# A trunk layer's first projections on one core: the first adaLN columns computed by TensorE, six places for w_ada, smaller first blocks, and ScalarE copies out of PSUM

## The chip, the cores and the metric

The kernel runs on one core of one Trainium2 chip. Its time is the device time of one execution in microseconds (us); the figure given is the median of three. Engines are named as in the profile: PE is TensorE's matmul, PEld its weight load, DVE is VectorE, ACT ScalarE, POOL GpSimd and SP SyncE, which here issues the loads.

## The reference, cut to what matters

The layer takes x (512 rows of 2048) and one conditioning vector c of 2048. Scale and shift columns come from c, and everything starts from them:

```python
cond = silu(c)
mod = cond @ w_ada + b_ada                  # 6 vectors of 2048
sh1, sc1, g1, sh2, sc2, g2 = split(mod, 6)
u = x * (1 + sc1) + sh1
proj = u @ w_in                             # 2048 -> 6168 columns: GLA and mLSTM
...                                         # the two head groups, w_out, LayerNorm, MLP, LayerNorm
```

Both head groups, the output projection and the MLP follow; the change doesn't touch them.

## The kernel before, in words

All matrices are f32. To keep precision, an operand is split into a high part (rounded to the reduced f32 format, tile names ending in h) and a low part (the remainder, ending in l), and a product is three matmuls: high by high, low by high, high by low.

The first stage computes five groups of 512 output columns (gla q, gla k, two halves of gla v, mLSTM q; numbered g = 0 to 4) while the adaLN columns are still being made. The contraction over 2048 is cut into 16 steps k of 128, and these into blocks, `KBLOCKS = (1, 2, 3, 4, 4, 2)`. The fifth group takes part in the first `XBLOCKS = 3` blocks (k = 0 to 5) only. For each block the kernel needs sc1 and sh1 for the block's k, so it works as follows, in the order in which it is written:

- `ada_start` loads the block's columns of x into one of the y tiles, and rows of the transposed w_ada: for each k and each of sc1 and sh1 two tiles of 128x1024. These go through `ring_b`, a ring of `RING = 4` places, three loads ahead. `ada_sum` (line 162) multiplies such a tile by silu(c), which `csb` holds in all 128 partitions, and sums along the row, on VectorE. `mod_cols` (lines 168 and 169) adds halves and bias for the whole block.
- `x_T` transposes x on TensorE; `u_tile` makes u^T on ScalarE (uf, line 341; its high part uh, line 125) and its low part ul on VectorE (line 126).
- `start_unit` loads a unit of w_in (two k of one group, 128x2x512; one k where a block is odd) into one of three places, has ScalarE cast it (line 138) and GpSimd make the low part (line 139): the split. The raw place is free when the split is done.
- TensorE multiplies a unit into four PSUM banks of the group; six banks rotate. After a block's last unit of a group, `start_evac` empties the banks. For the first block it copies to SBUF (ScalarE, for g = 3 VectorE, line 652); for later blocks VectorE adds the bank to what is in SBUF (line 654), 20 adds of 128x512 in a block of five groups, 16 in one of four.

In this stage ScalarE, VectorE and SP keep the order in which the code is written; TensorE and GpSimd get theirs from a scheduler when the program is built. The steps of the next block's `ada_start` are spread over the units of the block that runs, and the code ahead of the last unit finishes them, so that every u tile of a block waits for the sums of all of its k.

Loads of the gate columns and their split stand at the blocks that `GBLOCK` names, and are at k = 3 and k = 6 before and after the change within one block. Behind this stage come the other projections (`group`), with the GLA work between.

Of the kernel before, what the change touches and what calls it, by code (L numbers as in the profile page):

```python
# [33 lines left out]
KBLOCKS = (1, 2, 3, 4, 4, 2)  # L34
XBLOCKS = 3
KX = sum(KBLOCKS[:XBLOCKS])
GBLOCK = 2
# [21 lines left out]
def trunk_layer_kernel(  # L59
    ctx: ExitStack, tc: tile.TileContext,  # L60
    x, c, w_ada, b_ada, w_in, w_alpha, b_alpha, gla_g, conv_w, conv_b,
# [283 lines left out]
    def ada_start(k0, nk):  # L345
        xb = y[1 + len(xbn) % 3].rearrange("p (t c) -> p t c", c=CB)
        nc.sync.dma_start(xb[:, :, :nk * P], xr[:, :, k0 * P:(k0 + nk) * P])
        xbn.append(k0)
        xbs.update((k0 + i, (xb, i)) for i in range(nk))
        todo = [(v, k, h) for k in range(k0, k0 + nk) for v in (SC1, SH1) for h in range(2)]  # L350
        raws = [ada_load(*u) for u in todo[:RING - 1]]
        yield
        for i, u in enumerate(todo):
            ada_sum(raws.pop(0), *u)
            if i + RING - 1 < len(todo):
                raws.append(ada_load(*todo[i + RING - 1]))
            yield
        mod_cols(slice(SH1, SC1 + 1), k0, nk)
# [281 lines left out]

    def start_evac(i, g, j, bank):
# [1008 lines left out]
```

## Time and profile before

| what | us |
| --- | --- |
| median of three executions (2177.06 to 2185.43) | 2181.04 |
| the profiled execution | 2177.7 |
| its span, first to last instruction | 2176.0 |
| TensorE busy in it | 2116.9 |
| VectorE busy | 1753.3 |
| ScalarE busy | 949.7 |
| GpSimd busy | 164.7 |

The profile shows one execution. An engine's busy time is an average over stages with different limits: what a change in one stage can be worth is to be looked for in the idle time of TensorE in that stage. The granted clock of TensorE is given as a share of its full speed.

### The profile page before, as it was taken

The page shows a single profiled execution, that of the slowest core. Times are in us where ns is not written, and L with a number is a line of the kernel's source. Part 1 is how long each engine was busy: PE and PEld are TensorE (multiplying, and loading weights), DVE is VectorE, ACT ScalarE, POOL GpSimd, SP SyncE. Part 2 cuts the span into 40 slices and gives each one's busy share as a digit, 9 for nine tenths or more (in the row PEclk, how much of TensorE's full clock was granted, in tenths as well). Part 3 has the DMA queues.
Part 4 walks back from the last instruction along what each step waited for, and adds up shares of the span by engine and source line. Part 5 has one row for each costly group of instructions (what it writes and reads, how often), then busy time and mean ns, then how long its engine had stood idle before and what let it go on. Part 6 is the DMA issues. An engine that isn't in the chain of part 4 may idle for free.

```text
span 2176.0 us, 34974 instructions
## 1 busy us (share of the span) xinstructions
PE 2116.9 (97%) x13873; PEld 1929.2 (89%) x13873; DVE 1753.3 (81%) x2802; ACT 949.7 (44%) x1343; POOL 164.7 (8%) x151
## 2 busy tenths in 40 slices
PE   6989999999999999999999999999999999999997
PEld 4767788888887878999999999998999999998885
DVE  7986777677776878988788788789898988885888
ACT  4222644243332136454444454455555555554223
POOL 3334100000000000000000000000001001011002
PEclk9999999999999999999999999999999999999999
DMA  8885444666668857444444444355556766779852
GB/s 311 274 279 185 126 138 149 224 227 218 216 233 301 284 198 233 136 138 143 127 131 133 125 137 135 117 161 180 198 168 169 197 165 172 193 185 270 284 189 82
DMA packets 187087, 409.79 MB, mean 188 GB/s; under 512 B 17440, under 2 KB 19708, under 8 KB 186924
## 3 DMA queue, kind: packets, MB, share of 16 engines
q1 hardware_dynamic: 180588, 387.38, 54.6%
q0 software_dynamic: 6336, 20.19, 5.3%
q8 instruction: 108, 1.77, 0.3%
q14 instruction: 55, 0.45, 0.1%
HBM read 354.74 MB, written 52.71 MB: 187 GB/s over the span
## 4 chain that ended last, share of the span: by engine, by line
PE 74%; DVE 13%; DMA 8%; ACT 2%; issue 2%; POOL 0%; SPq 0%; ACTq 0%; DVEq 0%; POOLq 0%
PE fp L1362 8%; PE fp L1361 8%; PE fp L1363 8%; PE gp L1434 7%; PE gp L1435 7%; PE gp L1436 7%; DVE wr L162 3%; DMA wr<-in_w_ada_dram 3%; DMA f<-in_w_ff_dram 2%; PE wo_0b L228 1%; PE wo_0b L230 1%; PE wo_0b L229 1%; DMA q<-sums 1%; PE mv0b L228 1%; PE gr0b L228 1%
## 5 line engine op out<-in xcount | busy, mean ns | idle before, releaser
L162 DVE SCALAR_TENSOR_TENSOR wr<-wr,csb 128x1024 f32<-128x1024 f32 x192 | 255.5, 1352 | 25.8 <-DMA wr<-in_w_ada_dram 25.6
L1164 DVE TENSOR_TENSOR z<-f 128x512 f32<-128x512 f32 x208 | 142.4, 685 | 0.2 <-DMA f<-in_w_ff_dram 0.2
L1460 POOL DMA_DIRECT2D sums<-z x33 | 28.5, 867 | 1110.3 <-DVE f_10lo L1198 802.2
L1166 DVE TENSOR_TENSOR z<-f,z 128x256 f32<-128x256 f32 x208 | 88.4, 425 | 7.2
L1167 DVE TENSOR_TENSOR z<-f,z 128x256 f32<-128x256 f32 x208 | 88.4, 425 | 7.2
L1387 ACT ACTIVATE z<-z 128x1024 f32<-128x1024 f32 x28 | 28.1, 1052 | 58.1 <-DVE z L1382 58.1
L1457 ACT COPY z<-gp 128x512 f32<-128x512 f32 x90 | 45.5, 603 | 5.8 <-DMA sums<-z 4.8
L1194 ACT CAST f_6hi<-z 128x1024 fp32r<-128x1024 f32 x18 | 18.9, 1052 | 39.3 <-DVE z L1167 39.3
L1198 DVE TENSOR_TENSOR f_0lo<-z,f_0hi 128x1024 fp32r<-128x1024 f32 x17 | 20.8, 1226 | 18.5 <-ACT f_0hi L1194 18.5
L1194 ACT CAST f_4hi<-z 128x1024 fp32r<-128x1024 f32 x18 | 19.1, 1059 | 33.8 <-DVE z L1167 33.8
L1194 ACT CAST f_0hi<-z 128x1024 fp32r<-128x1024 f32 x17 | 17.8, 1050 | 33.3 <-PE fp L1362 24.5
L654 DVE TENSOR_TENSOR gqk<-gqk,st 128x512 f32<-128x512 f32 x40 | 25.3, 680 | 7.5 <-PE st L223 7.4
L1198 DVE TENSOR_TENSOR f_1lo<-z,f_1hi 128x1024 fp32r<-128x1024 f32 x14 | 17.2, 1226 | 17.6 <-ACT f_1hi L1194 17.6
L654 DVE TENSOR_TENSOR gv<-gv,st 128x512 f32<-128x512 f32 x40 | 25.2, 679 | 6.3 <-PE st L230 6.3
L832 ACT ACTIVATE y<-mo,dd 128x256 f32<-128x256 f32 x16 | 7.6, 475 | 51.9 <-DVE dd L825 51.9
L1391 ACT ACTIVATE z<-z 128x1024 f32<-128x1024 f32 x28 | 28.0, 1049 | 0.0
L1194 ACT CAST f_5hi<-z 128x1024 fp32r<-128x1024 f32 x14 | 14.7, 1051 | 30.4 <-DVE z L1167 30.4
L1194 ACT CAST f_1hi<-z 128x1024 fp32r<-128x1024 f32 x14 | 14.7, 1049 | 29.7 <-PE fp L1362 24.5
L1194 ACT CAST f_7hi<-z 128x1024 fp32r<-128x1024 f32 x14 | 14.7, 1050 | 28.8 <-PE fp L1362 24.4
L1198 DVE TENSOR_TENSOR f_6lo<-z,f_6hi 128x1024 fp32r<-128x1024 f32 x18 | 22.1, 1226 | 5.8 <-ACT f_6hi L1194 5.8
L1198 DVE TENSOR_TENSOR f_2lo<-z,f_2hi 128x1024 fp32r<-128x1024 f32 x18 | 22.1, 1225 | 5.8 <-ACT f_2hi L1194 5.8
L126 DVE TENSOR_TENSOR ul<-uf,uh 128x512 fp32r<-128x512 f32 x16 | 11.9, 752 | 18.2 <-ACT uh L125 18.2
(1914 smaller groups left out, 9015.6 us busy)
## 6 DMA issues: line engine op xcount, KB each, us to landing
f<-in_w_ff_dram SPq DMA_DIRECT2D x232, 512.0 KB, 3.8
wr<-in_w_ada_dram SPq DMA_DIRECT2D x192, 512.0 KB, 4.8
sums<-z POOLq DMA_DIRECT2D x33, 512.0 KB, 9.3
hd<-z SPq DMA_DIRECT2D x32, 512.0 KB, 4.0
z<-hd SPq DMA_DIRECT2D x28, 512.0 KB, 4.8
q<-sums SPq DMA_DIRECT2D x28, 256.0 KB, 5.9
sums<-z SPq DMA_DIRECT2D x12, 512.0 KB, 4.6
z<-in_x_dram SPq DMA_DIRECT2D x4, 1024.0 KB, 5.1
```

The costliest lines, as they stand in the source:

```text
L162: V.scalar_tensor_tensor(raw, raw, 1.0, csb[:, h * DH:(h + 1) * DH], ALU.mult, ALU.mult, accum_out=msum[:, h, v * KT + k:v * KT + k + 1])
L1164: V.tensor_tensor(halves(f[:, :S]), halves(raw[:, HB:3 * HB]), b12.unsqueeze(1).to_broadcast([P, 2, HB]), ALU.add)
L1166: V.tensor_tensor(t2, b22, n1, ALU.add)
L1167: V.tensor_tensor(t4, b21, t2, ALU.add)
L1194: A.copy(th, f)
L1198: V.tensor_tensor(tl, f, th, ALU.subtract)
L1361: T.matmul(o, lhsT=wh[:, sl], rhs=q[:, 0], start=i == 0 and j == 0, stop=False)
L1362: T.matmul(o, lhsT=wh[:, sl], rhs=q[:, 1], start=False, stop=False)
L1363: T.matmul(o, lhsT=wl[:, sl], rhs=q[:, 0], start=False, stop=i == KP - 1 and j == 1)
L1434: T.matmul(o, lhsT=qh[:, sl], rhs=wh, start=first and j == 0, stop=False)
L1435: T.matmul(o, lhsT=qh[:, sl], rhs=wl, start=False, stop=False)
L1436: T.matmul(o, lhsT=ql[:, sl], rhs=wh, start=False, stop=last and j == 1)
```

## The change

Five things change, all in the first stage.

1. The columns for k = 0 come from TensorE. The host passes `w_first`, the 2x128 columns of w_ada (not transposed) that give sh1 and sc1 for k = 0. c is loaded as 16 rows of 128, transposed, and passed through silu to `cs`; `ada_first` then does 2 x 16 plain f32 matmuls with one moving column each, and one VectorE add of the bias. `csb` is loaded later, behind the first two weight units, by `load_c`.
2. w_ada tiles have six places instead of four: `ring_s` adds two halves of the tile y[3], and five loads run ahead instead of three. x then uses two of the y tiles instead of three.
3. `KBLOCKS` becomes (1, 1, 2, 2, 4, 4, 2) with `XBLOCKS = 4`: k = 0 to 5 are four blocks instead of three, and five groups with 20 adds are emptied once more.
4. In all blocks but the first and the last, and for all groups but the block's last, ScalarE copies a bank into an SBUF tile (se, from the ring of `TB = 6` places that uf uses too), and VectorE adds that tile later (`start_adds`, line 677), ahead of the next unit's matmuls in the order of the code. 72 such copies are made.
5. `GBLOCK` becomes 3, which keeps the gate loads near the same k.

```diff
-KBLOCKS = (1, 2, 3, 4, 4, 2)
-XBLOCKS = 3
+KBLOCKS = (1, 1, 2, 2, 4, 4, 2)
+XBLOCKS = 4
...
-GBLOCK = 2
+GBLOCK = 3
...
+    rows_c = const.tile([KT, P], F32, name="rows_c")
+    nc.sync.dma_start(rows_c, c.rearrange("o (j p) -> (o j) p", p=P))
+    ctp = aux_bank("ctp")
+    T.transpose(ctp[:, :KT], rows_c, ident[:KT, :KT])
+    cs = const.tile([P, KT], F32, name="cs")
+    A.activation(cs, ctp[:, :KT], AF.Silu)
     csb = side.tile([P, D], F32, name="csb")
     DH = D // 2
-    for h in range(2):
-        nc.sync.dma_start(csb[:, h * DH:(h + 1) * DH],
-                          c[0:1, h * DH:(h + 1) * DH].broadcast_to([P, DH]))
-        A.activation(csb[:, h * DH:(h + 1) * DH], csb[:, h * DH:(h + 1) * DH], AF.Silu)
+
+    def load_c():
+        for h in range(2):
+            sl = slice(h * DH, (h + 1) * DH)
+            nc.sync.dma_start(csb[:, sl], c[0:1, sl].broadcast_to([P, DH]))
+            A.activation(csb[:, sl], csb[:, sl], AF.Silu)
...
-    def ada_load(v, k, h):
-        raw, r0 = ring_b(f"wr{v}_{k}_{h}"), (v * KT + k) * P
+    def ada_load(v, k, h, raw=None):
+        raw, r0 = raw or ring_b(f"wr{v}_{k}_{h}"), (v * KT + k) * P
...
-    def ada_start(k0, nk):
-        xb = y[1 + len(xbn) % 3].rearrange("p (t c) -> p t c", c=CB)
+    def x_load(k0, nk):
+        xb = y[1 + len(xbn) % 2].rearrange("p (t c) -> p t c", c=CB)
...
+    def ada_first():
+        tp, raws = aux_bank("mp"), []
+        for r in range(4):
+            raw = ring_b(f"wf{r}").rearrange("p (t c) -> p t c", c=2 * P)
+            nc.sync.dma_start(raw, w_first[r * CB:(r + 1) * CB].rearrange("(t p) c -> p t c", p=P))
+            raws.append(raw)
+        for v in range(2):
+            for k in range(KT):
+                T.matmul(tp[:, v:v + 1], lhsT=raws[k // 4][:, k % 4, v * P:(v + 1) * P],
+                         rhs=cs[:, k:k + 1], start=k == 0, stop=k == KT - 1)
+        V.tensor_tensor(mod[:, 0:2 * KT:KT], tp[:, :2], cA[:, 0:2 * KT:KT], ALU.add)
...
+    def ring_s():
+        ringn.append(len(ringn) % 6)
+        i = ringn[-1]
+        return y[3][:, (i - 4) * DH:(i - 3) * DH] if i > 3 else None
+
+    def ada_start(k0, nk):
+        x_load(k0, nk)
         todo = [(v, k, h) for k in range(k0, k0 + nk) for v in (SC1, SH1) for h in range(2)]
-        raws = [ada_load(*u) for u in todo[:RING - 1]]
+        raws = [ada_load(*u, ring_s()) for u in todo[:5]]
         yield
         for i, u in enumerate(todo):
             ada_sum(raws.pop(0), *u)
-            if i + RING - 1 < len(todo):
-                raws.append(ada_load(*todo[i + RING - 1]))
+            if i + 5 < len(todo):
+                raws.append(ada_load(*todo[i + 5], ring_s()))
             yield
...
+    adds = []
+
+    def start_adds():
+        while adds:
+            o, tmp = adds.pop(0)
+            V.tensor_tensor(o, o, tmp, ALU.add)
+
...
         if i == 0:
             (V.tensor_copy if g == 3 else A.copy)(o, src)
+        elif g == groups(i) - 1 or i == len(blocks) - 1:
+            V.tensor_tensor(o, o, src, ALU.add)
         else:
-            V.tensor_tensor(o, o, src, ALU.add)
+
+            tmp = tt2k(f"se{i}_{g}_{j}")
+            if 2 <= g < 4:
+                tmp = heads(tmp)
+            A.copy(tmp, src)
+            adds.append((o, tmp))
...
-    gen = ada_start(*blocks[0])
-    next(gen)
+    x_load(*blocks[0])
     tps = [x_T(k, mm_bank) for k in range(KBLOCKS[0])]
-    for _ in gen:
-        pass
+    ada_first()
     start_unit(0)
     start_unit(1)
+    load_c()
     for k, tp in enumerate(tps):
         u_tile(k, tp)
...
         for _ in range(share):
             next(gen, None)
+        start_adds()
```

Three places in the order of instructions. The first is ScalarE at the very start, up to the high part of the first u; cs is the small silu, csb the silu over all partitions, sw_0 the first weight units. Before:

```order
L98 ACT_TABLE_LOAD
L98 ACTIVATE csb<-csb 128x1024 x2
L138 CAST sw_0h<-sw_0r 128x512 x2
L341 ACTIVATE uf_170<-up_145,mod 128x512
L125 CAST uh_172<-uf_170 128x512
```

Now:

```order
L97 ACT_TABLE_LOAD
L97 ACTIVATE cs<-ctp 128x16
L145 CAST sw_0h<-sw_0r 128x512 x2
L105 ACTIVATE csb<-csb 128x1024 x2
L348 ACTIVATE uf_204<-up_141,mod 128x512
L132 CAST uh_206<-uf_204 128x512
```

The two passes over csb moved from the front to behind the first two weight casts, and still stand ahead of uf.

The second is VectorE where mod for k = 6 to 9 is made, at the end of the block with k = 5; gv is the running sum of the value projection, ul the low parts for k = 6 to 9. Before:

```order
L162 SCALAR_TENSOR_TENSOR wr_9_1_845,msum<-wr_9_1_845,csb 128x1024
L168 TENSOR_TENSOR mod<-msum 128x2x4
L169 TENSOR_TENSOR mod<-mod,cA_c 128x2x4
L126 TENSOR_TENSOR ul_944<-uf_941,uh_943 128x512
L126 TENSOR_TENSOR ul_955<-uf_952,uh_954 128x512
```

Now:

```order
L175 TENSOR_TENSOR mod<-msum 128x2x4
L176 TENSOR_TENSOR mod<-mod,cA_c 128x2x4
L677 TENSOR_TENSOR gv_104<-gv_104,se_2_0_1019 128x2x256
L677 TENSOR_TENSOR gv_105<-gv_105,se_2_1_1021 128x2x256
L677 TENSOR_TENSOR gv_106<-gv_106,se_2_2_1023 128x2x256
L677 TENSOR_TENSOR gv_107<-gv_107,se_2_3_1025 128x2x256
L677 TENSOR_TENSOR gv_104<-gv_104,se_3_0_1069 128x2x256
L677 TENSOR_TENSOR gv_105<-gv_105,se_3_1_1071 128x2x256
L677 TENSOR_TENSOR gv_106<-gv_106,se_3_2_1073 128x2x256
L677 TENSOR_TENSOR gv_107<-gv_107,se_3_3_1075 128x2x256
L133 TENSOR_TENSOR ul_1089<-uf_1086,uh_1088 128x512
```

The adds of groups 2 and 3 now stand between mod and the first ul; before, those groups were added ahead of mod.

The third is ScalarE inside a block (before the one with k = 3 to 5, now the one with k = 2 and 3); sw_2, sw_3, sw_4 and sw_5 are weight units, se the new SBUF tiles. Before:

```order
L125 CAST uh_583<-uf_581 128x512
L138 CAST sw_5h<-sw_5r 128x512
L138 CAST sw_3h<-sw_3r 128x1024
L138 CAST sw_5h<-sw_5r 128x512
L138 CAST sw_3h<-sw_3r 128x1024
```

Now:

```order
L145 CAST sw_2h<-sw_2r 128x1024
L698 COPY se_1_0_681<-st_1_0_653 128x512
L698 COPY se_1_1_683<-st_1_1_654 128x512
L698 COPY se_1_2_685<-st_1_2_655 128x512
L698 COPY se_1_3_687<-st_1_3_656 128x512
L145 CAST sw_2h<-sw_2r 128x1024
L698 COPY se_2_0_730<-st_2_0_702 128x512
```

Between two casts of weight units there are now four copies out of PSUM. Behind the first stage the instructions of each engine stand in the order in which they stood.

## Rows read from the trace of the kernel before

**Rows 1.** The page's head, and the busy time of each engine.

```profile
span 2176.0 us, 34974 instructions
PE 2116.9 (97%) x13873; PEld 1929.2 (89%) x13873; DVE 1753.3 (81%) x2802; ACT 949.7 (44%) x1343; POOL 164.7 (8%) x151
```

**Rows 2.** Busy us by stretch: PE, PEld, DVE, ACT, POOL; then PEclk, DMA share, GB/s.

```profile
0.00:18.23 18.23, 1.51 (x5) 0.90 (x5) 7.56 (x14) 6.08 (x8) 4.68 (x20) 1.00 0.92 332
...
18.23:124.06 105.83, 93.81 (x396) 73.94 (x397) 93.61 (x126) 34.76 (x52) 41.40 (x19) 0.97 0.84 285
124.06:179.80 55.74, 52.03 (x230) 39.26 (x229) 46.89 (x65) 17.33 (x23) 24.24 (x10) 1.00 0.78 270
...
179.80:227.00 47.20, 47.20 (x214) 38.19 (x213) 25.29 (x34) 12.51 (x15) 20.36 (x9) 1.00 0.38 122
```

**Rows 3.** Timeline up to the first projection: start, duration, instruction, idle before.

```profile
6.65 1.06 ACT L98 ACTIVATE csb<-csb 128x1024 f32<-128x1024 f32 x1 [0.74 <-DMA csb<-in_c_dram]
...
13.45 1.29 ACT L138 CAST sw_0h<-sw_0r 128x512 fp32r<-128x512 f32 x2 [5.74 <-DMA sw_0r<-in_w_in_dram]
...
16.75 0.78 ACT L341 ACTIVATE uf<-up,mod 128x512 f32<-128x512 f32 x1 [2.01 <-DVE mod L169]
...
18.23 0.80 PE L221 MATMUL st<-uh,sw_0h 128*128 128x512 f32 x1 [9.45 <-ACT uh L125]
```

**Rows 4.** Weight loads of transposes (ns min/median/max), and one plain f32 matmul's pair.

```profile
L335 PEld LDWEIGHTS up<-ident,y x20: 139/141/230, 7.7 to 46.4; 128*128 128x128 f32 x20
...
267.67 0.33 PE L577 MATMUL gs<-y,k 128*64 128x64 f32 x2
```

**Rows 5.** VectorE from 40.9 to 120 us: busy, mean ns, idle before.

```profile
L162 DVE SCALAR_TENSOR_TENSOR wr<-wr,csb 128x1024 f32<-128x1024 f32 x28 | 47.2, 1721 | 5.8 <-DMA wr<-in_w_ada_dram 5.8
L654 DVE TENSOR_TENSOR gv<-gv,st 128x512 f32<-128x512 f32 x16 | 9.9, 677 | 0.0
L654 DVE TENSOR_TENSOR gqk<-gqk,st 128x512 f32<-128x512 f32 x16 | 9.9, 675 | 0.0
L168 DVE TENSOR_TENSOR mod<-msum 128x6 f32<-128x6 f32 (+1 forms) x2 | 4.4, 2214 | 0.1
L654 DVE TENSOR_TENSOR y<-y,st 128x512 f32<-128x512 f32 x4 | 2.5, 681 | 0.0
...
L126 DVE TENSOR_TENSOR ul<-uf,uh 128x512 fp32r<-128x512 f32 x3 | 2.0, 688 | 0.6 <-ACT uh L125 0.6
```

**Rows 6.** Lines 654 and 162: ns min/median/max, first and last start.

```profile
L654 DVE TENSOR_TENSOR gqk<-gqk,st x40: 674/679/689, 46.5 to 241.8; 128x512 f32<-128x512 f32 x40
...
L162 DVE SCALAR_TENSOR_TENSOR wr<-wr,csb x28: 1211/1214/3409, 40.9 to 116.2; 128x1024 f32<-128x1024 f32 x28
```

**Rows 7.** Timeline of VectorE at single places.

```profile
40.91 1.22 DVE L162 SCALAR_TENSOR_TENSOR wr<-wr,csb 128x1024 f32<-128x1024 f32 x1 [2.50 <-DMA wr<-in_w_ada_dram]
...
46.55 2.47 DVE L654 TENSOR_TENSOR gqk<-gqk,st 128x512 f32<-128x512 f32 x4
48.94 1.21 DVE L162 SCALAR_TENSOR_TENSOR wr<-wr,csb 128x1024 f32<-128x1024 f32 x1
50.08 1.21 DVE L162 SCALAR_TENSOR_TENSOR wr<-wr,csb 128x1024 f32<-128x1024 f32 x1
...
121.44 0.69 DVE L126 TENSOR_TENSOR ul<-uf,uh 128x512 fp32r<-128x512 f32 x1 [1.55 <-ACT uh L125]
...
164.32 0.17 DVE L169 TENSOR_TENSOR mod<-mod,cA_c 128x8 f32<-128x8 f32 x1
```

**Rows 8.** SP's timeline between the first and the second wave of w_ada loads.

```profile
25.50 8.12 SPq L130 DMA_DIRECT2D sw_1r<-in_w_in_dram  x3
```

**Rows 9.** Timeline of TensorE: after a wait, and at k = 6.

```profile
56.40 0.80 PE L228 MATMUL st<-sw_1h,uh 128*128 128x512 f32 x1 [3.37 <-DVE gqk L654]
...
59.55 0.46 PE L229 MATMUL st<-sw_1l,uh 128*128 128x512 f32 x1
...
124.06 0.40 PE L221 MATMUL st<-uh,sw_6h 128*128 128x512 f32 x1
```

More of the change, by code (lines that the diff above doesn't have):

```diff
@@ L60, in trunk_layer_kernel @@
     ctx: ExitStack, tc: tile.TileContext,
-    x, c, w_ada, b_ada, w_in, w_alpha, b_alpha, gla_g, conv_w, conv_b,
+    x, c, w_ada, w_first, b_ada, w_in, w_alpha, b_alpha, gla_g, conv_w, conv_b,
     b_i, b_f, ml_g, w_out, ln1_g, ln1_b, w_ff1, w_ff2, ln2_g, ln2_b, out,
@@ L349, in ada_start @@
         xbs.update((k0 + i, (xb, i)) for i in range(nk))
+    def ada_first():
[9 more added lines that the diff above has]
+        V.tensor_tensor(mod[:, 0:2 * KT:KT], tp[:, :2], cA[:, 0:2 * KT:KT], ALU.add)
+    ringn = []
+    def ring_s():
[4 more added lines that the diff above has]
+        x_load(k0, nk)
         todo = [(v, k, h) for k in range(k0, k0 + nk) for v in (SC1, SH1) for h in range(2)]
-        raws = [ada_load(*u) for u in todo[:RING - 1]]
+        raws = [ada_load(*u, ring_s()) for u in todo[:5]]
         yield
@@ L1619, in trunk_layer_kernel @@
     f1p.release()
-_INS = ["x", "c", "w_ada", "b_ada", "w_in", "gla_w_alpha_up", "gla_b_alpha", "gla_norm_g",
+_INS = ["x", "c", "w_ada", "w_first", "b_ada", "w_in", "gla_w_alpha_up", "gla_b_alpha", "gla_norm_g",
         "mlstm_conv_w", "mlstm_conv_b", "mlstm_b_i", "mlstm_b_f", "mlstm_norm_g", "w_out",
         "ln1_g", "ln1_b", "w_ff1", "w_ff2", "ln2_g", "ln2_b"]
-_DROP = ("x", "w_ada", "w_in", "gla_w_alpha_up", "mlstm_conv_w", "w_out", "w_ff1", "w_ff2")
+_DROP = ("x", "w_ada", "w_first", "w_in", "gla_w_alpha_up", "mlstm_conv_w", "w_out", "w_ff1", "w_ff2")
 def kernel(**inputs):
@@ L1635 @@
     for name in _INS:
-        a = np.asarray(inputs[name])
+        a = np.asarray(inputs["w_ada" if name == "w_first" else name])
         if name in _DROP:
@@ L1640 @@
             a = a.T
+        if name == "w_first":
+            a = np.concatenate([a[:, :P], a[:, SC1 * D:SC1 * D + P]], 1)
         a = np.ascontiguousarray(a)
```

## The prediction, made before the changed kernel was timed

> **What bounds the kernel now.** I read the page's head first, then busy time by stretch, then the timelines of the stretches in which TensorE is not full. The profiled execution took 2177.7 us, its span is 2176.0 us, and TensorE is busy for 97% of it [rows 1]. No change can give more than the stretch that it touches loses, so the stretches come next [rows 2]. I cut them where TensorE takes up a new block of the contraction: 18.23 (k = 0), 124.06 (k = 6, the first matmul with tile sw_6h [rows 9]) and 179.80 (k = 10). Up to 18.23 TensorE has 1.5 us of work. From 18.23 to 124.06 it has 93.81 us of work in 105.83, from 124.06 to 179.80 52.03 in 55.74, and from 179.80 to 227 it is full: a loss of 16.7, 12.0, 3.7 and 0 us. The change rewrites only these stretches; the instructions behind them stand in the same order on every engine.
>
> The middle loss belongs to VectorE. It is busy 93.61 of the 105.83 us [rows 2]. There TensorE waits because VectorE, which works strictly in order, has not yet multiplied out the adaLN columns of the next block (the sums, line 162) or has not yet emptied a PSUM bank (the adds, line 654). What counts is when VectorE finishes mod for k = 6 to 9: in the kernel before 119.89, which is the start of ul at 121.44 less its wait of 1.55 [rows 7].
>
> **The start.** In the kernel before, the loads land in the order of their issue: both halves of csb (1.05 MB) by 6.65, the first weight tile by 13.45 when 3.67 MB have landed [rows 3], so 2.62 MB in 6.8 us, 0.385 MB a microsecond. In the changed kernel the four w_first tiles end at 2.41 MB: 6.65 + 1.36/0.385 = 10.2. Two chains then lead to the first projection.
> - *The columns.* The matmuls of ada_first run through all k for the first column, then again for the second. When the last tile lands, 4 + 16 matmuls are left. A matmul of plain f32 is two passes (a pair of records for one of line 577), and with one moving column a pass is little more than its load of 128 weight columns, of which the first transposes show 0.139 to 0.230 us [rows 4]. Forty passes are 5.6 to 9.2 us, so the sums are ready at 15.8 to 19.4. With 0.25 us for the add and 1.48 us from uf to the first matmul (16.75 to 18.23 [rows 3]) TensorE starts at 17.5 to 21.1.
> - *ScalarE's order.* The two passes over csb now stand ahead of uf, and csb lands behind 3.98 MB: 13.45 + 0.31/0.385 = 14.3. With 1.06 us for its last pass and 1.48 as above, 16.8.
>
> The first chain ends last. I take 18.5, nearer to its low end since 24 passes run ahead of those forty and may have brought the engine to its fast clock: no gain against 18.23. The Trainium skill (TensorE: Matmul & The Clock Gate, section LDWEIGHTS) has the load of 128 weight columns at 0.107 us whatever streams through them. By that the forty passes take 4.3 us, an estimate from that page, and the start would be 16.8, set by csb; the trace's weight loads here are 139 to 230 ns.
>
> **VectorE's ledger up to mod for k = 6 to 9.** In both kernels VectorE's steady work begins with the sums of the second load wave. Before, that is 40.91, after a wait of 2.50 [rows 7]: SP stood at three weight tiles for 8.12 us, until 33.62, and issued those w_ada loads behind them [rows 8], so they landed 7.3 us after it came free. What SP stands for is the GpSimd split of block 0's fifth unit. Afterwards that unit's load no longer queues behind busy w_ada buffers, and the split ends once TensorE is through two groups and ScalarE has copied and cast: 8 to 10 us after TensorE's start, 26.5 to 28.5, and with 7.3 33.8 to 35.8: **34.5** (31 to 36). Prices: a sum 1.14 us from start to start (48.94 to 50.08), four adds 2.39 (46.55 to 48.94), 0.60 each [rows 7].
> - *Before*, 40.91 to 119.89, 79.0 us [rows 5]: 28 sums, 32; 36 adds (16 + 16 + 4), 21.6; 3 ul, 2.0; 2 mod pairs, 0.7; waits 5.8 + 0.6. What is left, 17 us, is stall: the 28 sums took 47.2 us where 28 of 1.21 are 34.0, and the two mod adds 4.4 where undisturbed ones take 0.2 each. A stalled sum lasts up to 3.41 us [rows 6], 2.1 more than a free one, once for almost each of GpSimd's splits of 128x1024 that runs beside it.
> - *After*, the same point: 32 sums (blocks k = 2, 3; 4, 5; 6 to 9), 36.6; **48 adds** (20 + 20 + 8: the finer blocks empty the banks one round more often), 28.8; 4 ul, 2.6; 3 mod pairs, 1.0. That is 69.0 against 56.3.
> - *Stalls after*: 10 splits of 128x1024 (those of blocks k = 2, 3 and 4, 5) fall in this time, at 2.05 us 20.5; four of 128x512 are left out (up to 1 us each). The row for line 654 tells what is new here: an add with one operand in PSUM was never stalled (674 to 689 ns in 40 [rows 6]), and SBUF-only operations were. The change makes 40 of the 48 adds SBUF-only. If they stay free as before, stalls fall only on the sums, 36.6/(36.6 + 28.8) of 20.5: 11. I take 20.5, since a two-SBUF operand is what sums and adds then share. The Trainium skill (GPSIMD Engine Reference, section 1) says the same: GpSimd's SBUF interfaces are shared with VectorE and contend with instructions that read two SBUF inputs. By that rule the sum stands at 20.5; without it, it would be 11, and this rule speaks against the fourth part of the change.
> - *Waits after*: six places instead of four let SP run ahead, but the first wave is paced by landings: 3 (0 to 8).
>
> 34.5 + 69.0 + 20.5 + 3 = **127.0** for mod, against 119.9. From mod to the first ul VectorE then has eight adds first (two groups are pending, as the order rows show): 4.8 + 0.7, so TensorE starts k = 6 in earnest at 132.5. Before it started at 124.06, without a wait. That is **+8.4**.
>
> **After k = 6.** TensorE lost 3.7 us here. The adds for groups 0 to 2 no longer hold a bank: 12 copies of 0.6 us go to ScalarE, which is busy 17.33 of 55.74 [rows 2], and the six SBUF places behind the six banks cover the eight or nine sums in front of an add. **-3.7.** For k = 10 the lateness goes no further: before, its mod was there at 164.49 [rows 7], 15 us ahead of TensorE at 179.80. A gap of some us ahead of k = 6 also lowers TensorE's clock: after the wait that ended at 56.40 seven matmuls took 3.15 us to start where 1.6 is usual [rows 9], **+1.5**. ScalarE's 72 new copies (0.6 us each, 43 us up to k = 14) cost nothing: it works 52 of the 161 us up to 179.80; without that cover they would cost those 43. The loads of x into two buffers instead of three, the c rows and the late csb load cost nothing, being behind or ahead of loads that VectorE reaches later.
>
> **Sum**: 8.4 - 3.7 + 1.5 = +6.2 on the profiled execution's 2177.7, 2184. The median shown, 2181.0, is 3.3 above it, and the prediction is for a median: **2187 us**. A difference below 0.5% (10.9 us) is about what a measurement of this kernel can't tell from no change.
>
> **Rivals.**
> 1. *The ledger holds* (0.58): +6, 2187; its own range 2178 to 2196.
> 2. *The adds don't meet the splits* (0.20). Stalls 11, waits 0, start 33: mod at 113, TensorE at k = 6 at 118.5, that is -5.6; with -3.7, 2172. For it: the adds come in fours just after ScalarE's copies, and the split for the next group starts at about the same time and is soon over. Against it: SBUF-only ul and gw rows are stalled now. TensorE's own work forbids more than 18.5 + 93.8 = 112.3, -11.8 - 3.7, 2165.
> 3. *A loop closes, and it is slower* (0.22). ScalarE's copy waits for one of six SBUF places, so for VectorE's add; the cast of the next weight tile stands behind the copy, GpSimd's split behind the cast, SP's next weight load behind the split, and the next block's w_ada loads behind that. Before, no cast stood behind an add of VectorE on ScalarE's queue. It decides once VectorE runs so late that those loads land after it wants them; I put the slack at 4 us at k = 4 to 9. Price of one turn: the SP stand of 8.12 us [rows 8]. Mod at 135, TensorE at k = 6 at 140.5: +16.4 - 3.7 + 1.5 = +14, 2195. For it, VectorE is late by 7 already; against it, six places hold a group and a half.
>
> **The numbers.** The likeliest case gives 2187. The lower bounds together (31 + 69 + 11 + 0) and the upper ones (36 + 69 + 25 + 8 = 138, +17 in all) are unlikely to meet. The range that leaves out 2 in 10 is 2172 to 2200. Faster by over 0.5% needs 2170, the outer half of rival 2: 0.08. Slower by over 0.5% needs 2192: most of rival 3 and the upper tail of the ledger, 0.26. Within: 0.66.
>
> **What would show it.** Right: the first projection near 18.5; 108 adds in all on VectorE, and long ones (over 1 us) among those that read se tiles; mod for k = 6 to 9 near 127; TensorE idle ahead of k = 2, 4 and 6 with VectorE's ul as the one that ends it; no PSUM waits from there to k = 10. Wrong: adds on se tiles all near 680 ns (rival 2); ScalarE's copies waiting for adds, then SP for GpSimd's splits, then VectorE for w_ada (rival 3); a first projection after 21, with one-column passes above 0.23 us, which would move everything behind it; or TensorE waiting for ScalarE's casts between groups, which I have not priced.

## The result, and the profile after

The changed kernel took 2195.99 us (median; 2194.66 to 2197.50) against 2181.04 before: the ratio is 1.0075, 95% interval 1.0062 to 1.0087, so 16.4 us slower (13.5 to 19.0), clear of the 0.5% bound. The two medians as they stand differ by 15.0, which lies inside that interval. The prediction was 2187 in 2172 to 2200: the range holds it, the sign is right, and the time is 9 us above it. Its profiled execution has a span of 2195.2, 19.2 above that of before; that of before was 3.3 us under its median and this one 1.0 above, so the difference of these two executions overstates the change by about 4 us. The first fence is the page's head and the busy time by engine, the second the same view as [rows 2], cut where TensorE takes up k = 0, 6, 10 and 14.

```profile
span 2195.2 us, 35231 instructions
...
PE 2133.6 (97%) x13938; PEld 1946.2 (89%) x13938; DVE 1769.9 (81%) x2815; ACT 988.5 (45%) x1416; POOL 167.4 (8%) x151
```

```profile
0.00:22.68 22.68, 16.32 (x73) 15.23 (x73) 0.69 (x5) 6.26 (x9) 4.71 (x20) 1.00 0.81 268
22.68:140.08 117.40, 96.81 (x393) 76.68 (x394) 108.71 (x149) 59.67 (x100) 41.58 (x19) 0.94 0.79 277
140.08:197.04 56.96, 51.18 (x230) 39.59 (x228) 54.16 (x65) 22.86 (x34) 27.70 (x10) 1.00 0.71 249
197.04:244.26 47.22, 47.22 (x214) 38.22 (x212) 26.57 (x34) 19.25 (x27) 19.27 (x8) 1.00 0.30 91
```

Against [rows 2] the first projection is 4.45 us later (22.68 for 18.23), k = 6 is 16.0 later (140.08 for 124.06), k = 10 17.2 (197.04 for 179.80); the next stretch is as long as before. The loss lies ahead of k = 6, where VectorE is busy 108.71 of 117.40 us. The last 2 us of the 19.2 lie behind k = 14, in work that the change doesn't touch: 1950.9 us here, 1949.0 before, and 1945.5 (a_coarse) to 1952.5 (a_nofirst) in kernels below that have the same code there. So 2 us lie within what single executions show, and I don't explain them.

The start: TensorE's and its weight loads' timeline from 7 us on, then the instructions up to the first projection.

```profile
7.15 13.73 PEld L367 LDWEIGHTS mp<-cs,wf 128*128 128x128 f32 x64 [1.85 <-issue]
7.18 13.78 PE L367 MATMUL mp<-cs,wf 128*128 128x1 f32 x64 [1.48 <-DMA wf<-in_w_first_dram]
...
15.88 5.45 SPq L165 DMA_DIRECT2D wr<-in_w_ada_dram  x4
...
21.01 0.16 DVE L369 TENSOR_TENSOR mod<-mp,cA_c 128x2 f32<-128x2 f32 x1 [16.87 <-PE mp L367]
21.20 0.78 ACT L348 ACTIVATE uf<-up,mod 128x512 f32<-128x512 f32 x1 [4.50 <-DVE mod L369]
...
22.68 0.80 PE L228 MATMUL st<-uh,sw_0h 128*128 128x512 f32 x1 [0.97 <-ACT uh L132]
...
24.53 8.81 SPq L137 DMA_DIRECT2D sw_1r<-in_w_in_dram  x3
```

The 64 one-column passes run back to back from 7.15 to 20.9, 13.73/64 = 0.215 us each. No load paces them once the first tile is there. SP meanwhile stands 5.45 us, until 21.33, because these tiles hold four of the w_ada places, and the next weight loads go out behind that. It stands again until 33.34 for the split of a weight tile, ahead of the second wave's loads.

VectorE's timeline at the places of [rows 7]: the first sum of the second wave, and mod for k = 6 to 9 and k = 10 to 13.

```profile
41.16 1.77 DVE L169 SCALAR_TENSOR_TENSOR y<-y,csb 128x1024 f32<-128x1024 f32 x1 [2.94 <-DMA y<-in_w_ada_dram]
...
133.64 0.17 DVE L176 TENSOR_TENSOR mod<-mod,cA_c 128x8 f32<-128x8 f32 x1
...
184.02 0.17 DVE L176 TENSOR_TENSOR mod<-mod,cA_c 128x8 f32<-128x8 f32 x1
```

VectorE by line, from its first sum of the second wave to mod for k = 6 to 9 (the view of [rows 5]):

```profile
L169 DVE SCALAR_TENSOR_TENSOR wr<-wr,csb 128x1024 f32<-128x1024 f32 x20 | 34.3, 1759 | 0.0
L169 DVE SCALAR_TENSOR_TENSOR y<-y,csb 128x1024 f32<-128x1024 f32 x12 | 19.2, 1622 | 4.1 <-DMA y<-in_w_ada_dram 4.1
L677 DVE TENSOR_TENSOR gqk<-gqk,se 128x512 f32<-128x512 f32 x24 | 17.1, 771 | 0.0
L677 DVE TENSOR_TENSOR gv<-gv,se 128x512 f32<-128x512 f32 x16 | 14.2, 956 | 0.0
L692 DVE TENSOR_TENSOR y<-y,st 128x512 f32<-128x512 f32 x8 | 4.9, 670 | 0.0
```

And the lengths of the adds of line 677 in all (ns, minimum, median, maximum, as in [rows 6]), with who waited for them:

```profile
L677 DVE TENSOR_TENSOR gqk<-gqk,se x40: 676/679/2864, 47.4 to 219.6; 128x512 f32<-128x512 f32 x40
L677 DVE TENSOR_TENSOR gv<-gv,se x32: 677/682/2896, 58.1 to 230.5; 128x512 f32<-128x512 f32 x32
...
who waited for it (us, times):
  ACT se L698: 18.6, 6
```

The forecast's ledger can be read off: 32 sums and 24 + 16 + 8 = 48 adds, as counted. Nine sums lasted 1.77 to 3.42 us, 15.8 more than nine of 1.21; three of the 40 adds on se tiles 2.86 to 2.90, 6.6 more in all: stalls of 22 us. The adds on se tiles do meet the splits; the eight that read PSUM (line 692) show no stall.

What TensorE waited for, up to 320 us (total, times, longest):

```profile
PE st L235 <- ACT se L698: 8.6, 2, 4.4
PE up L342 <- ACT uf L348: 6.9, 3, 4.0
PE st L228 <- ACT uh L132: 5.2, 3, 3.2
...
PE st L236 <- POOL sw_6l L146: 2.0, 1, 2.0
PE st L228 <- ACT se L698: 1.9, 3, 1.4
PE st L229 <- DVE ul L133: 1.9, 2, 1.7
```

In the kernel before, the same view has three lines of waits for VectorE's adds, 8.8 us:

```profile
PE st L228 <- DVE gqk L654: 5.1, 2, 3.4
PE st L228 <- DVE gv L654: 1.9, 1, 1.9
PE st L221 <- DVE gqk L654: 1.8, 2, 1.3
```

These are gone, and waits for ScalarE's copies (10.5 us) and for u (uf, uh, ul) stand in their place. The copies themselves waited 18.6 us for VectorE's adds (ACT se L698 above).

### The profile page after: what moved, and what is told of

It is laid out like the page before. It is cut to its first block, busy times and chain, and to the rows that moved or that the text cites. A ratio compares the mean times of both kernels' runs of the same rounds, so it can differ in the third digit from the quotient of the medians.

```text
span 2195.2 us, 35231 instructions
## 1 busy us (share of the span) xinstructions
PE 2133.6 (97%) x13938; PEld 1946.2 (89%) x13938; DVE 1769.9 (81%) x2815; ACT 988.5 (45%) x1416; POOL 167.4 (8%) x151
## 4 chain that ended last, share of the span: by engine, by line
PE 75%; DVE 13%; DMA 6%; ACT 2%; issue 2%; POOL 0%; SPq 0%; ACTq 0%; DVEq 0%; POOLq 0%
PE fp L1406 8%; PE fp L1407 8%; PE fp L1408 8%; PE gp L1480 7%; PE gp L1479 7%; PE gp L1481 7%; DVE wr L169 3%; DMA f<-in_w_ff_dram 1%; PE wo_0b L237 1%; PE wo_0b L235 1%; PE wo_0b L236 1%; DMA wr<-in_w_ada_dram 1%; DMA q<-sums 1%; DVE y L169 1%; DVE gqk L677 1%
## 5 line engine op out<-in xcount | busy, mean ns | idle before, releaser
L169 DVE SCALAR_TENSOR_TENSOR wr<-wr,csb 128x1024 f32<-128x1024 f32 x168 | 221.7, 1340 | 8.5 <-DMA wr<-in_w_ada_dram 8.5
L698 ACT COPY se<-st 128x512 f32<-128x512 f32 x72 | 39.4, 595 | 33.1 <-PE st L230 11.9
L169 DVE SCALAR_TENSOR_TENSOR y<-y,csb 128x1024 f32<-128x1024 f32 x20 | 35.2, 1789 | 4.1 <-DMA y<-in_w_ada_dram 4.1
L1243 DVE TENSOR_TENSOR f_0lo<-z,f_0hi 128x1024 fp32r<-128x1024 f32 x17 | 20.8, 1225 | 18.1 <-ACT f_0hi L1239 18.1
L677 DVE TENSOR_TENSOR gqk<-gqk,se 128x512 f32<-128x512 f32 x40 | 28.6, 766 | 4.6 <-ACT se L698 4.6
L677 DVE TENSOR_TENSOR gv<-gv,se 128x512 f32<-128x512 f32 x32 | 25.7, 866 | 6.8 <-ACT se L698 6.8
L1243 DVE TENSOR_TENSOR f_1lo<-z,f_1hi 128x1024 fp32r<-128x1024 f32 x14 | 17.2, 1225 | 17.0 <-ACT f_1hi L1239 17.0
L1243 DVE TENSOR_TENSOR f_6lo<-z,f_6hi 128x1024 fp32r<-128x1024 f32 x18 | 22.1, 1225 | 5.9 <-ACT f_6hi L1239 5.9
```

Of the source, the lines that this page charges most:

```text
L169: V.scalar_tensor_tensor(raw, raw, 1.0, csb[:, h * DH:(h + 1) * DH], ALU.mult, ALU.mult, accum_out=msum[:, h, v * KT + k:v * KT + k + 1])
L677: V.tensor_tensor(o, o, tmp, ALU.add)
```

## The experiments

Each kernel was timed in five rounds beside the kernel before. The table has the twelve and the two that they start from; its marks (us) are of one profiled execution each: the first projection, VectorE's first sum of the second wave, TensorE's first matmul with k = 6 and with k = 10. The last column is (ratio - 1) x 2181. An interval is about 3 us to each side (4 for b_dup, 5 for a_late), so differences between two rows are good to about 4. A mark is less sure than a time: the profiled execution of b_114 took 5.5 us more than that kernel's median, that of b_dup 2.6 more, that of before 3.3 less.

| kernel | start | wave | k = 6 | k = 10 | ratio (95%) | us |
| --- | --- | --- | --- | --- | --- | --- |
| before | 18.2 | 40.9 | 124.1 | 179.8 | | |
| changed | 22.7 | 41.2 | 140.1 | 197.0 | 1.0075 (1.0062 to 1.0087) | +16.4 |
| b_first: part 1 alone | 22.4 | 45.2 | 126.2 | 180.9 | 0.9990 (0.9976 to 1.0005) | -2.2 |
| b_six: part 2 alone | 17.3 | 38.3 | 114.5 | 177.1 | 0.9982 (0.9967 to 0.9996) | -3.9 |
| b_fine: parts 3, 5 alone | 17.6 | 34.9 | 136.9 | 196.8 | 1.0051 (1.0035 to 1.0067) | +11.1 |
| b_act: part 4 alone | 18.1 | 40.6 | 124.9 | 183.5 | 1.0003 (0.9988 to 1.0017) | +0.7 |
| a_coarse: all but 3, 5 | 22.3 | 44.2 | 128.4 | 187.0 | 1.0003 (0.9991 to 1.0016) | +0.7 |
| a_direct: all but 4 | 22.1 | 39.5 | 129.2 | 189.8 | 1.0044 (1.0030 to 1.0058) | +9.6 |
| a_nofirst: all but 1 | 18.2 | 35.7 | 135.9 | 192.8 | 1.0047 (1.0030 to 1.0063) | +10.3 |
| b_firstsix: parts 1, 2 | 22.0 | 44.1 | 120.9 | 179.3 | 0.9984 (0.9969 to 0.9999) | -3.5 |
| b_dup | 17.1 | 39.7 | 136.7 | 200.1 | 1.0059 (1.0041 to 1.0078) | +12.9 |
| b_114 | 17.0 | 34.2 | 129.0 | 189.7 | 1.0017 (1.0005 to 1.0029) | +3.7 |
| a_late | 22.3 | 43.6 | 144.7 | 204.1 | 1.0089 (1.0066 to 1.0113) | +19.4 |
| a_onein | 22.0 | 38.5 | 125.8 | 177.2 | 0.9978 (0.9965 to 0.9992) | -4.8 |

### One part alone

**b_first.** The diff's first part only, with ring and adds as before:

```diff
+    ada_first()
+    start_unit(0)
+    start_unit(1)
+    load_c()
```

> The kernel before with only the first part of the change: the columns for k = 0 by TensorE, csb loaded behind the first two weight units; four w_ada places, blocks (1, 2, 3, 4, 4, 2) and direct adds as before. Theory A (the late start is paid in full): in the changed kernel the first projection began at 22.68 instead of 18.23, and SP's stand ended 10.7 us after it, so VectorE's second wave is tied to it: first projection near 22.7, k = 6 near 128.5, time about 4.5 us above before, 2185. Rival (VectorE's ledger is what counts, and it does not begin with the first projection): k = 6 still near 124, time within 1.5 us of before.

-2.2 us (-5.2 to 1.1): nearer to the rival, though k = 6 lies between the two. The start was 4.2 late and k = 6 2.1, k = 10 1.1. VectorE's columns came 4.2, 4.0, 2.1 and 1.2 us later from block to block (36.23, 74.71, 121.82, 165.50): in this kernel it waits for w_ada (9.2 us between 18 and 140 before, 7.2 now), and those 2.0 us are about what the late start lost of its lateness up to k = 6.

**b_six.** The diff's second part only:

```diff
-        raws = [ada_load(*u) for u in todo[:RING - 1]]
+        raws = [ada_load(*u, ring_s()) for u in todo[:5]]
```

> The kernel before with only the second part: six places for w_ada, x in two tiles instead of three. Theory A (places are not what VectorE waits for): VectorE waited 5.8 us for w_ada between 41 and 120 and TensorE lost 12 us in 105.8; more places can take away at most those 5.8, so between 2175 and 2181. Rival (deeper prefetch puts the weight loads of w_in behind more w_ada loads in SP's queue, as the 10.75 us wait of a cast in the changed kernel suggests): 2 to 6 us slower than before.

-3.9, theory A. The gain was 9.5 us at k = 6, and most of it was given back ahead of k = 10, in one wait of TensorE for an add (its timeline):

```profile
157.70 1.39 PE L228 MATMUL st<-sw_6h,uh 128*128 128x512 f32 x2 [6.81 <-DVE gv L661]
```

VectorE's timeline shows why that add came so late. In its order the add stands right behind mod for k = 10 to 13, so behind all 16 sums of that block:

```profile
156.88 0.17 DVE L169 TENSOR_TENSOR mod<-mod,cA_c 128x8 f32<-128x8 f32 x1
156.96 2.47 DVE L661 TENSOR_TENSOR gv<-gv,st 128x512 f32<-128x512 f32 x4
```

**b_fine.** Third and fifth part only:

```diff
-KBLOCKS = (1, 2, 3, 4, 4, 2)
-XBLOCKS = 3
+KBLOCKS = (1, 1, 2, 2, 4, 4, 2)
+XBLOCKS = 4
...
-GBLOCK = 2
+GBLOCK = 3
```

> The kernel before with only the third and fifth part: blocks (1, 1, 2, 2, 4, 4, 2), five groups in the first four. Theory A (adds on VectorE are the price): 20 more adds of 0.60 us ahead of k = 6 on an engine that was 88% busy there, so mod for k = 6 to 9 about 12 us later than 119.9, and 8 to 12 us slower: 2189 to 2193. Rival (smaller blocks let TensorE take up columns sooner, which covers the adds): within 3 us of before.

+11.1, theory A. The last add of mod for k = 10 to 13 started 12.3 us later than before (176.64 for 164.32), which is 20 adds of 0.62; it was stalled itself and ended 14.4 later. TensorE's waits for adds rose, between 30 and 140 us, from 7.1 us in the kernel before to 17.5, of which these lines are 16.7:

```profile
PE st L228 <- DVE gqk L654: 11.3, 3, 5.5
PE st L228 <- DVE gv L654: 3.1, 2, 2.8
PE st L221 <- DVE gqk L654: 2.3, 2, 1.6
```

**b_act.** Fourth part only:

```diff
-            V.tensor_tensor(o, o, src, ALU.add)
+            A.copy(tmp, src)
+            adds.append((o, tmp))
```

> The kernel before with only the fourth part: ScalarE copies a bank into SBUF and VectorE adds that tile later, in all blocks but the first and last, all groups but the last. Theory A (the copies stand behind casts that wait for weight loads, and the adds are held up by GpSimd's splits): TensorE waits for copies as it did in the changed kernel (10.5 us up to k = 6), some of it in place of the 8.8 us that it waits for adds in the kernel before: 3 to 8 us slower, 2184 to 2189. Rival (banks come free sooner, as my prediction had it): the 3.7 us behind k = 6 come back and no wait for copies is seen: 2 to 6 us faster.

+0.7, between the two: TensorE waits 6.4 us for copies, as theory A had it, in place of the 8.8 for adds, so little changes.

The four sum to 5.7 us (good to about 6) where the whole change costs 16.4: in one kernel the parts cost about 11 more than apart.

### The change less one part

**a_coarse.** Blocks of before:

```diff
-KBLOCKS = (1, 1, 2, 2, 4, 4, 2)
-XBLOCKS = 4
+KBLOCKS = (1, 2, 3, 4, 4, 2)
+XBLOCKS = 3
...
-GBLOCK = 3
+GBLOCK = 2
```

> The changed kernel with the blocks of before, (1, 2, 3, 4, 4, 2) and five groups in three of them; the other three parts stay. Theory A (the finer blocks carry the whole loss): parts one, two and four alone gave -1, -4 and +1 us, so 2175 to 2181, about 16 us below the changed kernel. Rival (the parts hurt one another: one late start, copies behind casts and adds behind splits together): still 6 us or more above before, 2187 or later.

+0.7 (-2.0 to 3.5): theory A by the time, which the finer blocks taken away give back. The marks give back less: k = 10 is at 187.0, 10 us ahead of the changed kernel's and 7 behind that of before, and this execution was 3.5 us shorter than before's behind k = 14 (1945.5 for 1949.0).

**a_direct.** No copies:

```diff
-        elif g == groups(i) - 1 or i == len(blocks) - 1:
+        else:
             V.tensor_tensor(o, o, src, ALU.add)
-        else:
...
-            A.copy(tmp, src)
-            adds.append((o, tmp))
```

> The changed kernel without its ScalarE copies: all adds read PSUM, as before; the finer blocks, six places and the first columns by TensorE stay. Theory A (with finer blocks the number of adds on VectorE sets the time, whoever empties the banks): within 4 us of the changed kernel, 2192 to 2196. Rival (copies behind casts cost the 10.5 us that TensorE waits for them up to k = 6, and stalled adds another 7 us): 8 us or more faster than the changed kernel, 2188 or less.

+9.6, 7 us less than the changed kernel: between the two, nearer to the rival. The adds of this kernel, in the same view as line 677 above, are never stalled, and VectorE's columns for k = 10 to 13 were ready at 171.4 instead of 184.2:

```profile
L692 DVE TENSOR_TENSOR gqk<-gqk,st x48: 671/676/689, 42.9 to 251.8; 128x512 f32<-128x512 f32 x48
L692 DVE TENSOR_TENSOR gv<-gv,st x48: 668/679/690, 57.4 to 260.5; 128x512 f32<-128x512 f32 x48
```

The sums, too, are stalled less: the 60 of the first stage lasted 23 us more than 1.22 each, in the changed kernel 32. By the start and end times, 42 of these 96 adds ran beside a split, and none of them took longer than 690 ns. Of the adds on se tiles in the changed kernel 10 of 72 did, and five of these were held up, by as much as a sum.

**a_nofirst.** The columns for k = 0 by sums, csb first, all else as changed:

```diff
-    ada_first()
...
-    load_c()
+    gen = ada_start(*blocks[0])
+    next(gen)
```

> The changed kernel without its first part: the columns for k = 0 by VectorE's sums as before; six places, finer blocks and ScalarE copies stay. Theory A (the ledger's start is the step that failed: VectorE's second wave began at 41.16, not 34.5, because the first projection began at 22.68): first projection near 17.5, second wave near 36, k = 6 near 135 instead of 140.08, and 4 to 6 us faster than the changed kernel, 2190 to 2192. Rival (a late start is made up on the way, as in the kernel before, where the first part alone cost nothing): within 2 us of the changed kernel, 2194 to 2198.

+10.3, 6 us less: theory A. VectorE's timeline at the second wave and TensorE's at k = 6:

```profile
35.71 2.31 DVE L162 SCALAR_TENSOR_TENSOR wr<-wr,csb 128x1024 f32<-128x1024 f32 x1 [2.40 <-DMA wr<-in_w_ada_dram]
...
135.91 0.63 PE L221 MATMUL st<-uh,sw_6h 128*128 128x512 f32 x1
```

The late start isn't made up here: start, k = 6 and k = 10 differ from the changed kernel's by 4.5, 4.2 and 4.3 us. In both kernels VectorE waits for w_ada for only 4 us between 18 and 140.

**b_firstsix.** Parts one and two, with coarse blocks and adds from PSUM.

```diff
-KBLOCKS = (1, 1, 2, 2, 4, 4, 2)
-XBLOCKS = 4
+KBLOCKS = (1, 2, 3, 4, 4, 2)
+XBLOCKS = 3
...
-        elif g == groups(i) - 1 or i == len(blocks) - 1:
+        else:
             V.tensor_tensor(o, o, src, ALU.add)
-        else:
...
-            A.copy(tmp, src)
-            adds.append((o, tmp))
```

> The kernel before with parts one and two together: the first columns by TensorE and six w_ada places, with the blocks of before and all adds from PSUM. Theory A (the ScalarE copies cost about 6 us in the coarse kernel too, since parts one, two and four together came out at +1): -2 and -4 us add up, 2173 to 2178, faster than both kernels. Rival (one and two give the same time back, and the copies cost nothing with coarse blocks): 2179 to 2183.

-3.5, theory A by its number, and no more than part two alone. Whether the two gains add (to -6.1) these intervals don't tell. Against a_coarse, which has the copies too, it is 4.2 us less. This and b_six are the fastest versions that compute the whole reference, each 0.2% below the kernel before with an interval that just leaves out no change.

### The mechanisms by themselves

**b_dup.** Twenty more passes of VectorE, without finer blocks:

```diff
+            if i == 1:
+                V.tensor_scalar(bank, bank, 1.0, None, ALU.mult)
             V.tensor_tensor(o, o, src, ALU.add)
```

> The kernel before, coarse blocks, with 20 extra VectorE passes over a PSUM bank, times 1.0 in place, one ahead of each add of the block with k = 1 and 2: the work of one more round of adds without the round. Theory A (the 20 adds themselves are the price of finer blocks, 0.6 us each on the engine that is the bound): 8 to 13 us slower, 2189 to 2194, as with the finer blocks alone. Rival (the price is the added block boundary, where TensorE waits for columns, u and banks): less than 4 us slower.

+12.9, theory A. The passes took as long as adds:

```profile
L655 DVE TENSOR_SCALAR st<-st x20: 683/692/693, 45.4 to 90.4; 128x512 f32<-128x512 f32 x20
```

**b_114.** Small first blocks without more adds:

```diff
-KBLOCKS = (1, 2, 3, 4, 4, 2)
+KBLOCKS = (1, 1, 4, 4, 4, 2)
```

> The kernel before with blocks (1, 1, 4, 4, 4, 2): small first blocks, but as many blocks and adds as before. Theory A (the count of adds is the price, not the small blocks): within 5 us of before, 2176 to 2186. Rival (small early blocks leave TensorE too little work to cover the sums of the next block; here a block of one k, 13.6 us of matmuls, stands ahead of 16 sums of at least 1.14 us, 18 us): TensorE waits 8 us or more ahead of k = 2, and 6 us or more slower than before.

+3.7 (1.1 to 6.3), theory A by the time: something, but a third of the price of the added round. The rival's wait did come (TensorE stood 14.2 us for adds ahead of k = 2), but not its price.

**a_late.** Cast and split behind the copies:

```diff
+            casts.append((hi, lo, raw, m))
...
                 start_evac(i, g, j, banks[j])
+        start_cast()
```

> The changed kernel with the cast and the split of a weight unit written behind the ScalarE copies of the unit that runs, instead of ahead of them; the load stays where it is. No copy out of PSUM then stands behind a cast that waits for a load. Theory B (that order costs the time: TensorE waited 10.5 us for copies up to k = 6): those waits go, and 5 us or more faster than the changed kernel, 2191 or less. Theory C (VectorE is the bound, and what the copies cost is stalls: adds with both operands in SBUF beside GpSimd's splits): TensorE waits for u instead, within 3 us of the changed kernel, 2193 to 2199.

+19.4, at least no better than the changed kernel: the forecast of theory B fails, though the run puts other waits in the place of those that it takes away. TensorE's waits for copies go, and waits for ul (6.4 us), uh, casts and splits come. A cast now stands behind copies that wait for VectorE's adds (ScalarE from 22 to 145, idle time ahead of the copies and what ended it):

```profile
L710 ACT COPY se<-st 128x512 f32<-128x512 f32 x48 | 27.4, 590 | 57.2 <-DVE gqk L689 27.7 <-PE st L230 21.6 <-DVE gv L689 6.9
```

**a_onein.** GpSimd reads one operand instead of two:

```diff
-        pend.append(lambda: (eng or V).tensor_tensor(lo[:, :nt, :n], raw[:, :nt, :n],
-                                                     hi[:, :nt, :n], ALU.subtract))
+        pend.append(lambda: G.tensor_scalar(lo[:, :nt, :n], raw[:, :nt, :n], 0.0, None, ALU.mult) if eng
+                    else V.tensor_tensor(lo[:, :nt, :n], raw[:, :nt, :n], hi[:, :nt, :n],
+                                         ALU.subtract))
```

> The changed kernel with GpSimd's split of a weight unit replaced by a one-operand pass over the same tile: the low part is the raw tile times 0, so the low parts of the first stage's weights are left out of the product (TensorE's work stays). Theory C (VectorE is stalled because a GpSimd pass and a VectorE pass, each with two operands in SBUF, run side by side): none of VectorE's 128x1024 sums lasts over 1.3 us, no add over 0.8 us, the 22 us of stalls up to k = 6 go, and TensorE reaches k = 6 by 125: 8 us or more faster than the changed kernel. Rival (any GpSimd pass over SBUF stalls VectorE, or the stalls come from something else): sums of 2 us or more beside GpSimd's passes remain, and the time is within 5 us of the changed kernel.

-4.8: 21 us below the changed kernel. VectorE's sums up to 200 us and its adds (ns), and one group of GpSimd's passes:

```profile
L170 DVE SCALAR_TENSOR_TENSOR wr<-wr,csb x40: 1209/1214/2053, 22.6 to 189.9; 128x1024 f32<-128x1024 f32 x40
...
L678 DVE TENSOR_TENSOR gqk<-gqk,se x40: 676/680/1523, 44.8 to 199.8; 128x512 f32<-128x512 f32 x40
```

```profile
L146 POOL TENSOR_SCALAR sw_4l<-sw_4r 128x1024 fp32r<-128x1024 f32 x5 | 15.7, 3143 | 20.4 <-DMA sw_4r<-in_w_in_dram 11.4 <-PE up L343 4.8 <-issue 2.7
```

Theory C in its main point: the sums' excess over 1.22 us fell from 32 to 5 us, that of the 72 adds over 0.68 only from 9 to 7, and the time by 21. Not word for word: sums up to 2.05 and adds up to 1.53 us remain, so a one-operand pass stalls VectorE too, by 0.84 us instead of 2.2, though it lasts 3.1 us, longer than a split's 2.6 to 2.9 on the mean. The stalls didn't fall because passes met less often: by the start and end times, 77 of VectorE's sums and adds on se tiles ran beside a GpSimd pass here and 17 were held up, against 36 and 22 in the changed kernel. The pass no longer waits for the cast, so a part of the 21 us of time may come from that; this wasn't separated.

## Why the prediction was right or wrong

**The bound and the ledger: right.** VectorE's work ahead of mod for k = 6 to 9 was put at 69.0 + 20.5 + 3 = 92.5 us. It took 133.8 - 41.2 = 92.6, with 22.4 us of stalls, 1.2 of waits behind the first sum, and so 69 of work. That the total agrees to a tenth is luck: the stalls were 1.9 us more than forecast and the waits 1.8 less. b_fine and b_dup show that the added adds are the price, about 12 us. Two slips in the working change nothing: of the 79.0 us before, 16.3 are left for stalls and not 17 (79.0 - 56.3 - 6.4), and a stalled sum is 2.2 us longer than a free one, not 2.1 (3.41 for 1.21).

**The start: wrong, and this is the step that failed.** "I take 18.5, nearer to its low end since 24 passes run ahead of those forty and may have brought the engine to its fast clock" became 22.68, and with it "34.5 (31 to 36)" for the second wave became 41.16. Half of the 4.2 us is the price of a pass. The bracket held it (0.215 in 0.139 to 0.230), but 18.5 takes 0.164 of it ((18.5 - 1.73 - 10.2)/40), on the bet on the fast clock, and 40 x 0.051 is 2.0. The other half is the count: by 10.2, when the last tile was to land, only 14 passes could be done, since the first did not start before 7.15; fifty were left, not forty, and 64 x 0.215 behind 7.15 is 20.9. The second wave then lost 2.5 us more, most of it because SP's stand ended 10.7 us behind the first projection instead of 8 to 10, and the loads landed 7.8 behind it instead of 7.3. Nor did the unit's load stop queueing behind busy w_ada buffers: SP stood 5.45 us for them, until 21.33. a_nofirst, with its start at 18.2, has its second wave at 35.7, inside the 31 to 36 of the forecast; the ledger behind it held again (93.6 us to mod at 129.3). That step is worth 4 us by the marks and 6 (good to about 4) by the times.

**From mod to k = 6: right.** 5.5 was forecast, 6.3 measured.

**Behind k = 6: wrong in sign.** "-3.7" for bank waits that vanish, less 1.5 for the clock: the bank waits did vanish, but TensorE waited 5.8 us there for uf (2.9), a split (2.0) and a cast (0.9) instead. The 1.5 was not paid there: from 140.08 on, matmuls of 512 columns start 0.23 us apart, at a granted clock of 1.00; the clock was lower ahead of k = 6 (0.94 on the mean, 0.97 before).

```profile
PE up L342 <- ACT uf L348: 2.9, 2, 2.2
PE st L236 <- POOL sw_6l L146: 2.0, 1, 2.0
PE st L228 <- ACT sw_8h L145: 0.9, 1, 0.9
```

"For k = 10 the lateness goes no further" failed as well: mod for k = 10 to 13 came at 184.0, 19.7 later than before, ScalarE's uf stood for it, and TensorE's wait for uf is that lateness (ScalarE's timeline):

```profile
184.28 0.78 ACT L348 ACTIVATE uf<-up,mod 128x512 f32<-128x512 f32 x1 [5.68 <-DVE mod L176]
```

From k = 6 to k = 10 the changed kernel lost 1.2 us where a gain of 2.2 was forecast.

**The sum.** Of the 13 us between +6.2 and the +19.2 of the profiled execution, 7.6 lie ahead of k = 6 (6.7 of them the start of the second wave), 3.4 from there to k = 10, and 2 behind that. That the range held the time owes to its width, 28 us: the sum itself was less than half of what was measured.

**The rivals.** Rival 2 is refuted: the adds meet the splits, and the sums' stalls alone (15.8 us) are above its 11. Rival 3 named about the time, 2195, but not the cause: its loop needs VectorE to stand for late w_ada loads, and VectorE stood 4.1 us up to k = 6 in the changed kernel. Its first link is there (copies waited 18.6 us for adds), but the chain doesn't come back to VectorE. "ScalarE's 72 new copies cost nothing" holds of ScalarE's own time; still TensorE waited 10.5 us for copies, which themselves waited for adds, and the kernel without copies is 6.8 us faster.

**The rule on the shared interfaces.** With stalls on adds that read two SBUF operands the forecast had 20.5, without them 11; 22.4 were measured, and a_direct, whose adds read PSUM, removes those of the adds altogether. The Trainium skill (GPSIMD Engine Reference, section 1) has GpSimd's SBUF interfaces contend with VectorE instructions that read two SBUF inputs, and the trace agrees with that. The Trainium skill (SBUF — State Buffer, section SBUF: two separate sides) has the shared ports as a lock that one engine holds for its whole instruction while the other is blocked, against any GpSimd operation that reads SBUF. There a_onein differs: passes of 3.1 us with one operand held sums up by at most 0.84 us, and the measurement decides.

**What the finer blocks do, and what is left.** The finer blocks cost 11.1 us alone, 13.1 beside parts one and two (a_direct against b_firstsix) and 15.7 beside parts one, two and four (changed against a_coarse), each good to about 4: most of the 16.4 in every company. How the rest splits has no single answer, since the shares depend on which part is taken away first.

- *The first columns by TensorE* cost nothing in two pairs with coarse blocks (-2.2 against before, +0.4 for b_firstsix against b_six) and 6 us in the changed kernel against a_nofirst. Whether the finer blocks or the copies make that difference wasn't separated.
- *The copies* cost nothing alone (+0.7), 4.2 us beside parts one and two with coarse blocks (a_coarse against b_firstsix) and 6.8 with finer ones. The last two differ by less than the noise, so it isn't shown that finer blocks make the copies dearer.
- *Where a late start is given back.* It is tempting to say that the 20 adds take VectorE's slack, but its waits for w_ada don't show that: b_firstsix, with coarse blocks, has as few (4.1 us from 18 to 140). Its lateness against b_six was 6.4 us at k = 6 and 2.2 at k = 10, and 2.7 us of that difference is TensorE's wait for the add behind mod, 4.1 us instead of 6.8. The gain of part two at k = 6 is lost in the same wait. The changed kernel and a_nofirst show no wait for an add from k = 6 to k = 10, and there the late start stays (4.2 us at k = 6, 4.3 at k = 10). That it costs in full for this reason is argued from the traces; no run shows it by itself.

## What to carry to other kernels

When a strictly ordered engine bounds a stage, count its instructions first: here a finer blocking of the contraction bought no time and cost one more round of read-modify-write, 20 adds and 11 to 13 us. Price a change together with its companions: a late start that cost nothing in two pairs of kernels cost 6 us in a third. And when work is to be handed to an idle engine at the start, multiply the whole chain out from its first possible start, not only the part behind the last load, and don't take the low end of a bracket for its price without a row that shows it.

## What the runs showed of the hardware that I had not expected

A VectorE pass with two operands in SBUF was held up by as much as 2.2 us by a two-operand GpSimd pass of 2.6 to 2.9 us on the mean, and by at most 0.84 us by a one-operand pass of 3.1. An add with one operand in PSUM wasn't held up at all (668 to 690 ns in 96 adds, 42 of them beside a split).

The one-column matmuls, back to back from 7.15 to 20.9, didn't leave TensorE at its fast pace. The matmuls of 512 columns behind them start 0.43 us apart from 23.3 to 26.7, which is the lower of the two clock levels (512 columns at 1.2 GHz), and 0.23 apart from 27.1 on. In the kernel before, behind an idle time of 9.45 us [rows 3], they are as slow from 19.6 to 22.1. The granted clock stands at 1.00 in both stretches, so that column doesn't show it. Here is the changed kernel's timeline at that place.

```profile
25.84 0.63 PE L229 MATMUL st<-ul,sw_0h 128*128 128x512 f32 x1
26.26 0.63 PE L230 MATMUL st<-uh,sw_0l 128*128 128x512 f32 x1
26.69 0.57 PE L228 MATMUL st<-uh,sw_0h 128*128 128x512 f32 x1
27.10 0.39 PE L229 MATMUL st<-ul,sw_0h 128*128 128x512 f32 x1
27.33 0.40 PE L230 MATMUL st<-uh,sw_0l 128*128 128x512 f32 x1
```

So the one-column passes, 0.215 us apart, will have run at that slow pace too; no run has them at the other. The Trainium skill (TensorE: Matmul & The Clock Gate, section LDWEIGHTS) has 0.107 us for a load of 128 columns, half of what was measured.
